# Rotation tables loaded two samples sooner, parted sets ranked ahead, a head's finish one step later, and idle products among the first ones, in a one-core encoder layer

## The chip, the cores and the metric

One core of a Trainium2 chip runs the whole kernel. The metric is the device time of one execution in microseconds (us); the median of three runs is given. A profile of one such execution shows what every engine did: TensorE (PE: matrix products and transposes), VectorE (DVE), ScalarE (ACT), GpSimd (POOL) and SyncE (SP), which here only issues loads and stores.

## What is computed

One layer of a hybrid streaming encoder, for 512 prompt frames and 8 samples of 16 new frames (640 rows of 1024 channels), all in float32:

```
x = x + 0.5 * swiglu(rms_norm(x), ffn1)
z = rms_norm(x) @ w_in_mix            # rq rk rv rg | fq fk fv ff | gates
retention (4 heads): q, k rotated (rotary); o = decayed attention + q @ state; new state
FoX (8 heads): softmax attention with the logit bias sum log f; prompt in blocks of 128,
               samples against 1024 cached frames each
x = x + (g0 * (rms_norm(o_ret) * silu(rg)) @ w_br_ret + g1 * o_fox @ w_br_fox) @ w_out
x = x + 0.5 * swiglu(rms_norm(x), ffn2)
x = x + (p @ w_ple) * sigmoid(rms_norm(x) @ w_ple_gate)
```

## The kernel before

The rows are kept transposed, 640 of them beside each other. Large products are made from weights and inputs that are each split in two parts in a rounded format (ACT casts the first part, `wh`, at L282; DVE makes the rest, `wl`, at L283), as `wh` and `wl` products of 128 x 128 x 320 on PE, all issued by the helper `mm` (L205; transposes are L228). In the mixing part a product of a block of `w_in_mix` is a unit of seven such sums (`MixSeven`), which takes a tile `z1` at its third sum (L822) and `z0` at its fourth (L827), both with the tag `blk`, of which there are 38 slots; the finished rows go to DRAM (`zdram`, `vdram`) on POOL's queue.

These units are the filler. The kernel is written as one order: the mixer's own steps in their turn and, after each step, `fill(us)` issues so many microseconds (by a clock that is kept while the kernel is built) of unit products; `defer` puts a step some time later, `until` runs units up to a name, and `drain` runs all that are left. The builder's order of the instructions follows that order by rank, but takes what is ready. So the stages that matter are, by the time in the profiled execution: FFN 1 (0 to some 480 us); the FoX prompt sweep, `prompt_scores` (L1164) for 2 head groups x 2 pairs x 4 blocks (some 510 to 620); the samples, 8 x 8 steps (`Sample.step`, with its scores, softmax, flips, values and, last, `fold` at L1335 to L1342), to 832; the four retention heads (`Retention`, 832 to some 940, with units between), each with 12 steps; then what follows mixing.

What the change touches: `mm` and its neighbours (L205); the first loop of FFN 1 (`plain[0].products(norm1.ops, j)`, L698; `keep_busy(n, x)`, L253, issues n products of `ones` that nobody reads, into a bank of its own); `prompt_scores`, a set of four products for a pair of heads, two over 40 rows that spread the bias and two over 64 rows, side by side in the array; `Retention.values_s` (L1432), one product and eight over 32 columns each, into one PSUM bank; the sample loop (L1631) and the stretch behind it that loads the tables of retention: `tab` (two tables `c_rope` for `rotate`, L1374), `gqt`, `smt` (`c_smask`, for `scores_s`) and the masks; and `Retention.finish` (ten transposes, products at L1473 and L1474, two stores by POOL). `load` issues on SP's queue, not before a product that lies some time (30 us unless told) earlier by the kept clock.

A tile of a tag takes a slot in the order of the code, and a slot is free when the last reader of the tile before is done. `tmp`, `att`, `big` (in the trace `kv`) and `blk` are such tags in SBUF; `pa` and `pg` are PSUM banks.

Of the kernel before, what the change touches and what calls it, by code (L numbers as in the profile page):

```python
# [19 lines left out]
P = 128  # L20
# [3 lines left out]
NB = 8  # L24
L = 16
# [5 lines left out]
RH, DK, DV = 4, 128, 256  # L31
FH, FD = 8, 64
# [12 lines left out]
LEAD = 30.0  # L45

MERGE_THEN = 5, 1, 1, 0
FILL_P0, FILL_P1, FILL_S0, FILL_S, FILL_R, FILL_B = 1.76, 1.6, 19.8, 10.0, 2.45, 6.4

SM = {}  # L50
# [81 lines left out]
def kernel(  # L132
# [20 lines left out]
    def nm(base):  # L153
        uid[0] += 1
        return f"{base}_{uid[0]}"
# [3 lines left out]
    def blk(shape=(P, T), dt=F32, tag="blk"):  # L159
        n = 1  # L160
        for s in shape[1:]:
            n *= s
        assert n <= T
        return bp.tile(list(shape), dt, tag=tag, name=nm(tag), bufs=slots[tag])
# [4 lines left out]
    def att(dt=F32, shape=(P, 512)):  # L169
        return blk(shape, dt, tag="att")  # L170
# [10 lines left out]
    def tmp(shape=(P, H2), dt=F32):  # L181
        return bp.tile(list(shape), dt, tag="tmp", name=nm("tmp"), bufs=NTMP)
# [4 lines left out]
    def bank(tag="pa"):  # L187
        return pp.tile([P, 512], F32, tag=tag, name=nm(tag), bufs=6 if tag == "pa" else 2)

    def pair(tag="pa"):  # L190
        return [bank(tag), bank(tag)]
# [3 lines left out]
    def tick(inst, us):  # L195

        clock[0] += us
        if not issued or clock[0] - issued[-1][0] > 1.0:
            issued.append((clock[0], inst.ins.name))

    def mm(out, lhsT, rhs, start, stop, **kw):
        n = 1
        for d in rhs.shape[1:]:
            n *= d
        i = nc.tensor.matmul(out, lhsT, rhs, start=start, stop=stop, **kw)  # L205
        tick(i, max(n, 256) / 2400.0 if rhs.dtype == F32R else max(n, 128) / 600.0 * (0.3 if lhsT.shape[-1] <= 32 else 0.5 if lhsT.shape[0] == FD else 1.0))
        return i

    def after(inst, name, why):
        tc.add_manual_dep(inst.ins, name, mybir.DependencyInfo(mybir.DependencyClass.NoSync, mybir.DependencyReason.SCHED_ONLY), reason=why)  # L210

    def load(out, in_, lead=LEAD):

        i = nc.sync.dma_start(out, in_)  # L214
        at = clock[0] - lead
        name = next((nm_ for c, nm_ in reversed(issued) if c <= at), None)
        if name is not None:
            after(i, name, "no tile taken too soon")
# [22 lines left out]
    def flip_gains(n0, n, rows):  # L241
        gb, at = bank("pg"), slice(n0, n0 + n)
        transpose(gb[:, :n * KC], rows)
        nc.vector.tensor_copy(gains[:, at].rearrange("p n c -> p (n c)"), gb[:, :n * KC])
        nc.vector.tensor_scalar(less[:, at], gains[:, at], -1.0, None, op0=ALU.mult)
# [7 lines left out]
    def keep_busy(times, x=None):  # L253

        for _ in range(times):
            nc.tensor.matmul(busy[:, :P], ones, ones if x is None else x[:, :P], start=True, stop=True)
# [395 lines left out]
    with tc.manual_schedule(engines={mybir.EngineType.SP}):  # L652
        for q in range(KC // 2):
            cols = slice(q * 256, (q + 1) * 256)
            xi = big((P, TB, 256))
            n = P if q == 0 else 256
# [16 lines left out]
    xs0 = []  # L673

    def x_in(q):
        for c in (2 * q, 2 * q + 1):
            xc = blk()
            b, b2 = bank(), bank("pg")
            for t in range(TB):
                transpose(b[:, t * P:(t + 1) * P] if t < 4 else b2[:, :P], xins[q][:, t, c % 2 * P:(c % 2 + 1) * P])  # L680
            nc.vector.tensor_copy(xc[:, :S], b)
            nc.scalar.copy(xc[:, S:], b2[:, :P])
            if c == 0:
                keep_busy(4, xc)
            xs0.append(xc)
            norm1.add_parts(c, xc)
            if c % 2 == 0:
                first_parts(norm1.ops, xc[:, H2:], norm1.gain(c), "b12")

    def x_out(q):  # L690
        for c in (2 * q, 2 * q + 1):
            nc.sync.dma_start(xd[0][c], xs0[c])
        norm1.add_square(xins[q], marks[max(q - 1, 0)])

    plain, marks = [Plain(raws[0])], []
    for j in range(KC // 2):
        x_in(j)
        plain[0].products(norm1.ops, j)  # L698
        marks.append(issued[-1][1])
        if j:  # L700
            x_out(j - 1)
        if j == 2:
            flip_gains(1, 3, more)
# [56 lines left out]
    def defer(us, thunk):  # L760
        uid[0] += 1
        heapq.heappush(deferred, (clock[0] + us, uid[0], thunk))

    def pump(everything=False):
        while deferred and (everything or deferred[0][0] <= clock[0]):
            heapq.heappop(deferred)[2]()
# [177 lines left out]
    pick = const.tile([104, FH], F32R, name="pick")  # L944
    c_row = []
# [76 lines left out]
    qk_out = {}  # L1022
# [141 lines left out]
    def prompt_scores(hu, pr, i):  # L1164

        n, both = (i + 1) * P, pair()
        for h2, ps in ((1, both[1]), (0, both[0])):
            head, rows = hu * 4 + 2 * pr + h2, slice(h2 * FD, h2 * FD + 40)
            last = mm(ps[:, :n], pick[rows, head:head + 1].to_broadcast([40, P]), c_row[0][rows, :n], True, False, skip_group_check=True)
        for h2, ps in ((1, both[1]), (0, both[0])):  # L1170
            rows = slice(h2 * FD, (h2 + 1) * FD)
            m = mm(ps[:, :n], qk_out[hu][rows, 0, pr, i * P:n], qk_out[hu][rows, 1, pr, :n], False, True, skip_group_check=True)
            if h2 == 1:
                after(m, last.ins.name, "the pair of heads side by side in the array")
        while values_due:
            values_due.pop(0)(m)
        for h2, ps in enumerate(both):
            prompt_softmax(hu, 2 * pr + h2, i, n, ps)
# [167 lines left out]
    class Retention:  # L1346
# [85 lines left out]
        def values_s(self):  # L1432

            po = bank()
            mm(po[:, :DV], self.at_s, self.vs[4], True, False, skip_group_check=True)
            for j in range(2):
                for pr in range(NB // 2):
                    mm(po[pr * 32:(pr + 1) * 32, :DV], self.qg[:, pr, j, :], self.st[:, 2 * pr + j, :], False, j == 1, skip_group_check=True)
            o, sq = tmp([P, DV]), tmp([P, DV])
            nc.scalar.copy(o, po[:, :DV])  # L1440
            nc.scalar.activation(sq, o, AF.Square, accum_out=self.ms[:, 4:])
            self.o.append(o)
# [136 lines left out]
    merge[-1].begin, merge[-1].middle = embed_begin, fox_fetch  # L1579
    for hd, n in enumerate(MERGE_THEN):  # L1580
        units += [merge.pop(0) for _ in range(n)]
# [13 lines left out]
    def fill(us):  # L1595
        credit[0] += us
        while credit[0] > 0.0:
            at = clock[0]
            if next(feed, feed) is feed:
                clock[0] += credit[0]  # L1600
                credit[0] = 0.0
            credit[0] -= clock[0] - at
            pump()

    def until(what):
        while what not in ready:
            next(feed)
            pump()

    def drain():  # L1610
        for _ in feed:
            pump()
# [15 lines left out]
    samples[0].load(samples[0].k, cache_k)  # L1628
    samples[0].load(samples[0].k, cache_k)
    fill(FILL_B)  # L1630
    for b in range(NB):  # L1631
        defer(2.0, lambda: samples[b].loads(samples[b + 1] if b + 1 < NB else None))
        for n in range(8):
            samples[b].step(n)
            fill((FILL_S if b else FILL_S0) / 8)
    until("rk")
    fill(FILL_B)
    pump(True)
    tab = []
    for n in range(2):  # L1640
        r = blk()
        load(r, c_rope[n])
        tab.append(r)
    gqt, smt = tmp([P, RH, 2, 2 * L]), blk([P, RH, P])
    load(gqt, c_gq)
    load(smt, c_smask)
    masks = [att(shape=(P, RH, P)) for _ in range(2)]
    for n in range(2):
        load(masks[n], c_rmask[n])
    heads = [Retention(hd) for hd in range(RH)]  # L1650
# [3 lines left out]
    fill(6.0)  # L1654
    for hd, r in enumerate(heads):
        for step in (
            lambda: r.rotate(0), lambda: r.rotate(1), lambda: (r.flip(), heads[hd + 1].first_loads() if hd + 1 < RH else None),
            lambda: r.scores(), lambda: r.scores_s(),
            lambda: (r.states_p(), heads[hd + 1].loads() if hd + 1 < RH else None),
            lambda: r.values(0), lambda: r.values(1), lambda: (r.values_s(), r.states()),  # L1660
            lambda: (r.sizes(), until(("rg", hd)), r.gates()),
            lambda: heads[hd + 1].more_loads() if hd + 1 < RH else None, lambda: r.finish(),
        ):
            step()
            fill(FILL_R)
    drain()
    pump(True)

# [4 lines left out]
    for op in range(KC // 2):  # L1673
# [5 lines left out]
        for o in range(2):  # L1679
            n = 2 * op + o  # L1680
            ps = pair()
# [7 lines left out]
    for op in range(KC // 2):  # L1689
        raw = raw_unit(w_out[0][:, op * 256:(op + 1) * 256], KC, 256)  # L1690
        two = []
        for o in range(2):
            xc = blk()
            load(xc, spill[2 * op + o])
            ps = pair("pa")
# [14 lines left out]
    for q in range(2):  # L1710
        for t in range(TB):
            ps = bank("pa" if t % 2 else "pg")
# [23 lines left out]
    for q in range(4):  # L1736
# [15 lines left out]
        for t in range(TB):  # L1752
            ps = bank()
# [41 lines left out]
```

## Time and profile before

| | us |
| --- | --- |
| runs | 1625.13, 1622.28, 1623.24 |
| median | 1623.24 |
| profiled execution, its own time | 1622.67 |
| span of the profiled execution | 1620.9 |
| PE busy | 1609.3 |
| DVE busy | 1164.4 |
| ACT busy | 731.5 |

The span is the time from the first to the last recorded instruction; the execution's own time has some 1.8 us around it. Busy time is the union of an engine's instructions, whose ends on PE are modelled: a stretch at a lower clock counts as busy. The granted clock of PE (1.00 for 2.4 GHz, 0.50 for 1.2 GHz) is therefore read beside it, in windows of the trace. Waits name the instruction that came last before the waiting one could go on.

### The profile page before, as it was taken

How to read it: one execution, taken by the hardware profiler on the slowest of the kernel's cores; microseconds unless marked ns; L12 is line 12 of the kernel's file. 1: busy time of each engine (PE TensorE's matmuls, PEld its weight loads, DVE VectorE, ACT ScalarE, POOL GpSimd, SP SyncE). 2: the span in 40 equal slices, each digit the busy share in tenths (PEclk: the TensorE clock that was granted, in tenths of full speed). 3: DMA queues.
4: the chain of work that ended last, by engine and by line, in shares of the span. 5: the costliest groups of instructions: out<-in, count | busy, mean ns of one | idle time of the engine just before them, and what ended most of it. 6: DMA issues, size and time to landing. Idle time of an engine off the chain costs nothing.

```text
span 1620.9 us, 30289 instructions
## 1 busy us (share of the span) xinstructions
PE 1609.3 (99%) x11979; PEld 1557.3 (96%) x11979; DVE 1164.4 (72%) x2472; ACT 731.5 (45%) x1536; POOL 94.5 (6%) x172
## 2 busy tenths in 40 slices
PE   9999999999999999999999999999999999999998
PEld 8999999999999888988889999999999999999998
DVE  6885786577777755777779886558884787578663
ACT  6552354244454444444434454435653355235432
POOL 0000000000011111000000010001000000000000
PEclk9999999999999999999999999999999999999999
DMA  7244233433542333577775676444234333433431
GB/s 249 78 131 139 96 93 131 145 101 94 178 130 97 111 115 133 209 281 269 279 259 179 202 260 247 151 135 155 79 101 164 100 91 124 144 111 90 172 123 46
DMA packets 205566, 242.88 MB, mean 150 GB/s; under 512 B 10176, under 2 KB 175984, under 8 KB 201328
## 3 DMA queue, kind: packets, MB, share of 16 engines
q1 hardware_dynamic: 193824, 200.07, 38.0%
q0 software_dynamic: 11392, 40.79, 6.3%
q8 instruction: 94, 1.54, 0.4%
q14 instruction: 48, 0.39, 0.1%
q10 hardware_dynamic: 208, 0.08, 0.0%
HBM read 194.89 MB, written 46.03 MB: 149 GB/s over the span
## 4 chain that ended last, share of the span: by engine, by line
PE 96%; DMA 2%; DVE 1%; ACT 1%; issue 0%; SPq 0%; DVEq 0%
PE pa L205 74%; PE pg L205 18%; PE pa L228 4%; DMA kv<-zdram 1%; DMA blk<-in_c_rope_dram 0%; DMA raw<-in_ffn_w_in_dram 0%; ACT tmp L533 0%; PE pg L228 0%; DVE wl L283 0%; ACT wh L282 0%; DMA kv<-in_x_prompt_dram 0%; SPq L214 0%; DVE kv L1487 0%; ACT blk L361 0%; DVE blk L1473 0%
## 5 line engine op out<-in xcount | busy, mean ns | idle before, releaser
L282 ACT CAST wh<-raw 128x512 fp32r<-128x512 f32 (+1 forms) x525 | 316.3, 613 | 506.7 <-PE pa L205 323.5
L205 PE MATMUL pa<-blk,wh 128*128 128x320 f32 x2344 | 511.1, 311 | 1.1 <-ACT wh L282 1.0
L283 DVE TENSOR_TENSOR wl<-raw,wh 128x512 fp32r<-128x512 f32 (+1 forms) x525 | 351.0, 678 | 107.0 <-ACT wh L282 103.6
L205 PEld LDWEIGHTS pa<-blk,wh 128*128 128x128 f32 x2344 | 388.2, 189 | 4.5 <-ACT wh L282 1.5
L205 PE MATMUL pa<-blk,wl 128*128 128x320 f32 x1172 | 344.4, 310 | 0.0
L205 PE MATMUL pa<-kv,wh 128*128 128x320 f32 x1344 | 251.5, 308 | 0.0
L205 PEld LDWEIGHTS pa<-blk,wl 128*128 128x128 f32 x1172 | 216.5, 189 | 0.5 <-DVE blk L830 0.4
L205 PEld LDWEIGHTS pa<-kv,wh 128*128 128x128 f32 x1344 | 210.6, 188 | 0.0
L205 PE MATMUL pg<-blk,wh 128*128 128x320 f32 x768 | 177.3, 316 | 0.2 <-DVE blk L830 0.2
L205 PE MATMUL pa<-blk,blk 128*128 128x320 f32 (+2 forms) x1064 | 168.3, 304 | 0.0
L205 PE MATMUL pa<-kv,wl 128*128 128x320 f32 x672 | 154.6, 308 | 0.0
L205 PEld LDWEIGHTS pa<-blk,blk 128*128 128x128 f32 (+1 forms) x1064 | 151.9, 183 | 0.1
L205 PE MATMUL pg<-wh,blk 128*128 128x256 f32 x768 | 147.6, 286 | 0.0
L205 PEld LDWEIGHTS pg<-blk,wh 128*128 128x128 f32 x768 | 128.2, 188 | 6.0 <-issue 2.4
L205 PEld LDWEIGHTS pg<-wh,blk 128*128 128x128 f32 x768 | 120.4, 188 | 5.1 <-issue 3.8
L205 PE MATMUL pg<-blk,wl 128*128 128x320 f32 x384 | 118.7, 309 | 0.0
L205 PEld LDWEIGHTS pa<-kv,wl 128*128 128x128 f32 x672 | 112.6, 188 | 0.0
L205 PE MATMUL pg<-wl,blk 128*128 128x256 f32 x384 | 108.7, 284 | 0.0
L283 DVE TENSOR_TENSOR blk<-raw,blk 128x512 fp32r<-128x512 f32 x82 | 56.3, 688 | 38.3 <-ACT blk L282 28.0
L205 PE MATMUL pa<-wh,blk 128*128 128x256 f32 (+1 forms) x432 | 82.4, 285 | 0.0
L282 ACT CAST blk<-raw 128x512 fp32r<-128x512 f32 x82 | 50.7, 621 | 62.5 <-DMA raw<-in_ffn_w_in_dram 48.8
L205 PEld LDWEIGHTS pg<-wl,blk 128*128 128x128 f32 x384 | 72.1, 188 | 1.9 <-issue 1.3
(287 smaller groups left out, 2205.1 us busy)
## 6 DMA issues: line engine op xcount, KB each, us to landing
raw<-in_ffn_w_in_dram SPq DMA_DIRECT2D x86, 512.0 KB, 4.8
raw<-in_w_in_mix_dram SPq DMA_DIRECT2D x25, 1024.0 KB, 5.8
raw<-in_ffn_w_out_dram SPq DMA_DIRECT2D x16, 1024.0 KB, 5.2
kv<-in_cache_fox_k_dram SPq DMA_DIRECT2D x16, 1024.0 KB, 7.1
kv<-in_cache_fox_v_dram SPq DMA_DIRECT2D x16, 1024.0 KB, 5.6
blk<-xd SPq DMA_DIRECT2D x48, 320.0 KB, 5.7
xd<-blk POOLq DMA_DIRECT2D x40, 320.0 KB, 2.8
zdram<-blk POOLq DMA_DIRECT2D x24, 320.0 KB, 3.4
```

The source lines that it names most:

```text
L205: i = nc.tensor.matmul(out, lhsT, rhs, start=start, stop=stop, **kw)
L228: tick(nc.tensor.transpose(out, in_, ident[: in_.shape[0], : in_.shape[0]]), 0.11)
L282: nc.scalar.copy(hi, src)
L283: nc.vector.tensor_tensor(lo, src, hi, op=ALU.subtract)
```

## The change

Four things: a name `together()` for "rank what is issued here 300 places ahead", put around the four products of a set in `prompt_scores` and around the nine of `values_s`; eight idle products behind the first group of FFN 1's products; the two tables and `smt` loaded at the start of sample 6 of 0 to 7, and no longer after the last sample; and each head's `finish` issued in the second step of the next head (the last one's after the loop), so that a head has 11 steps with a fill behind each instead of 12.

```
--- before.py
+++ after.py
@@ -45,6 +45,7 @@
 LEAD = 30.0
 
 MERGE_THEN = 5, 1, 1, 0
+SET_AHEAD = 300
 FILL_P0, FILL_P1, FILL_S0, FILL_S, FILL_R, FILL_B = 1.76, 1.6, 19.8, 10.0, 2.45, 6.4
 
 SM = {}
@@ -205,6 +206,10 @@
         i = nc.tensor.matmul(out, lhsT, rhs, start=start, stop=stop, **kw)
         tick(i, max(n, 256) / 2400.0 if rhs.dtype == F32R else max(n, 128) / 600.0 * (0.3 if lhsT.shape[-1] <= 32 else 0.5 if lhsT.shape[0] == FD else 1.0))
         return i
+
+    def together():
+
+        return tc.high_priority(offset=SET_AHEAD)
 
     def after(inst, name, why):
         tc.add_manual_dep(inst.ins, name, mybir.DependencyInfo(mybir.DependencyClass.NoSync, mybir.DependencyReason.SCHED_ONLY), reason=why)
@@ -696,6 +701,8 @@
     for j in range(KC // 2):
         x_in(j)
         plain[0].products(norm1.ops, j)
+        if j == 0:
+            keep_busy(8, xs0[1])
         marks.append(issued[-1][1])
         if j:
             x_out(j - 1)
@@ -1164,14 +1171,15 @@
     def prompt_scores(hu, pr, i):
 
         n, both = (i + 1) * P, pair()
-        for h2, ps in ((1, both[1]), (0, both[0])):
-            head, rows = hu * 4 + 2 * pr + h2, slice(h2 * FD, h2 * FD + 40)
-            last = mm(ps[:, :n], pick[rows, head:head + 1].to_broadcast([40, P]), c_row[0][rows, :n], True, False, skip_group_check=True)
-        for h2, ps in ((1, both[1]), (0, both[0])):
-            rows = slice(h2 * FD, (h2 + 1) * FD)
-            m = mm(ps[:, :n], qk_out[hu][rows, 0, pr, i * P:n], qk_out[hu][rows, 1, pr, :n], False, True, skip_group_check=True)
-            if h2 == 1:
-                after(m, last.ins.name, "the pair of heads side by side in the array")
+        with together():
+            for h2, ps in ((1, both[1]), (0, both[0])):
+                head, rows = hu * 4 + 2 * pr + h2, slice(h2 * FD, h2 * FD + 40)
+                last = mm(ps[:, :n], pick[rows, head:head + 1].to_broadcast([40, P]), c_row[0][rows, :n], True, False, skip_group_check=True)
+            for h2, ps in ((1, both[1]), (0, both[0])):
+                rows = slice(h2 * FD, (h2 + 1) * FD)
+                m = mm(ps[:, :n], qk_out[hu][rows, 0, pr, i * P:n], qk_out[hu][rows, 1, pr, :n], False, True, skip_group_check=True)
+                if h2 == 1:
+                    after(m, last.ins.name, "the pair of heads side by side in the array")
         while values_due:
             values_due.pop(0)(m)
         for h2, ps in enumerate(both):
@@ -1432,10 +1440,11 @@
         def values_s(self):
 
             po = bank()
-            mm(po[:, :DV], self.at_s, self.vs[4], True, False, skip_group_check=True)
-            for j in range(2):
-                for pr in range(NB // 2):
-                    mm(po[pr * 32:(pr + 1) * 32, :DV], self.qg[:, pr, j, :], self.st[:, 2 * pr + j, :], False, j == 1, skip_group_check=True)
+            with together():
+                mm(po[:, :DV], self.at_s, self.vs[4], True, False, skip_group_check=True)
+                for j in range(2):
+                    for pr in range(NB // 2):
+                        mm(po[pr * 32:(pr + 1) * 32, :DV], self.qg[:, pr, j, :], self.st[:, 2 * pr + j, :], False, j == 1, skip_group_check=True)
             o, sq = tmp([P, DV]), tmp([P, DV])
             nc.scalar.copy(o, po[:, :DV])
             nc.scalar.activation(sq, o, AF.Square, accum_out=self.ms[:, 4:])
@@ -1628,7 +1637,15 @@
     samples[0].load(samples[0].k, cache_k)
     samples[0].load(samples[0].k, cache_k)
     fill(FILL_B)
+    tab = []
     for b in range(NB):
+        if b == NB - 2:
+            for n in range(2):
+                r = blk()
+                load(r, c_rope[n])
+                tab.append(r)
+            smt = blk([P, RH, P])
+            load(smt, c_smask)
         defer(2.0, lambda: samples[b].loads(samples[b + 1] if b + 1 < NB else None))
         for n in range(8):
             samples[b].step(n)
@@ -1636,14 +1653,8 @@
     until("rk")
     fill(FILL_B)
     pump(True)
-    tab = []
-    for n in range(2):
-        r = blk()
-        load(r, c_rope[n])
-        tab.append(r)
-    gqt, smt = tmp([P, RH, 2, 2 * L]), blk([P, RH, P])
+    gqt = tmp([P, RH, 2, 2 * L])
     load(gqt, c_gq)
-    load(smt, c_smask)
     masks = [att(shape=(P, RH, P)) for _ in range(2)]
     for n in range(2):
         load(masks[n], c_rmask[n])
@@ -1654,15 +1665,16 @@
     fill(6.0)
     for hd, r in enumerate(heads):
         for step in (
-            lambda: r.rotate(0), lambda: r.rotate(1), lambda: (r.flip(), heads[hd + 1].first_loads() if hd + 1 < RH else None),
+            lambda: r.rotate(0), lambda: (heads[hd - 1].finish() if hd else None, r.rotate(1)), lambda: (r.flip(), heads[hd + 1].first_loads() if hd + 1 < RH else None),
             lambda: r.scores(), lambda: r.scores_s(),
             lambda: (r.states_p(), heads[hd + 1].loads() if hd + 1 < RH else None),
             lambda: r.values(0), lambda: r.values(1), lambda: (r.values_s(), r.states()),
             lambda: (r.sizes(), until(("rg", hd)), r.gates()),
-            lambda: heads[hd + 1].more_loads() if hd + 1 < RH else None, lambda: r.finish(),
+            lambda: heads[hd + 1].more_loads() if hd + 1 < RH else None,
         ):
             step()
             fill(FILL_R)
+    heads[-1].finish()
     drain()
     pump(True)
```

## Rows read from the trace of the kernel before

**Rows 1.** The page: busy time of each engine over the whole span (us, share, instructions), and the chain of work that ended last, by engine.
```profile
PE 1609.3 (99%) x11979; PEld 1557.3 (96%) x11979; DVE 1164.4 (72%) x2472; ACT 731.5 (45%) x1536; POOL 94.5 (6%) x172
...
PE 96%; DMA 2%; DVE 1%; ACT 1%; issue 0%; SPq 0%; DVEq 0%
```

**Rows 2.** The waits of PE over the whole span: engine, tile and line, what was waited for, us in total, times, longest.
```profile
PE pa L205 <- DVE tmp L1335: 2.6, 1, 2.6
PE pg L228 <- DMA kv<-in_x_sample_dram: 1.5, 1, 1.5
...
PE pa L205 <- DVE blk L1473: 0.4, 1, 0.4
```

**Rows 3.** The chain that ended last, in order of time: start, us, what. The piece ahead of the products at 831.75.
```profile
822.05 7.81 DMA blk<-in_c_rope_dram
```

**Rows 4.** The timeline of DVE, 825 to 832 us: start, us, engine, line, operation, out<-in, count, and in brackets the idle time before it and what ended it.
```profile
825.19 0.69 DVE L424 TENSOR_TENSOR raw<-raw 128x512 f32<-128x512 f32 x1
829.88 1.56 DVE L1374 TENSOR_TENSOR kv<-kv,blk 128x640 f32<-128x640 f32 x2 [4.00 <-DMA blk<-in_c_rope_dram]
831.36 0.34 DVE L1335 SCALAR_TENSOR_TENSOR tmp<-pa,ty,sm 128x128 f32<-128x128 f32 x1
```

**Rows 5.** The timeline of PE, 828 to 834 us.
```profile
828.57 0.45 PE L205 MATMUL pg<-blk,wh 128*128 128x320 f32 x2
828.86 0.31 PE L205 MATMUL pg<-blk,wl 128*128 128x320 f32 x1
831.75 0.57 PE L205 MATMUL pa<-sm,tmp 128*128 128x64 f32 x2 [2.59 <-DVE tmp L1335]
...
833.04 0.73 PE L205 MATMUL pa<-blk,wh 128*128 128x320 f32 x2
833.57 0.47 PE L205 MATMUL pa<-blk,wl 128*128 128x320 f32 x1
```

**Rows 6.** Busy time of each engine in stretches of the span (in the columns after the length: busy us and instructions of PE, PEld, DVE, ACT and POOL; then the granted clock of PE, the DMA engines' busy share, GB/s).
```profile
13.00:14.00 1.00, 1.00 (x8) 1.00 (x6) 0.49 (x1) 1.00 (x7) 0.00 (x0) 0.50 1.09 377
760.00:770.00 10.00, 10.00 (x77) 8.93 (x76) 7.55 (x17) 5.38 (x14) 1.08 (x2) 1.00 0.55 179
815.00:832.00 17.00, 14.41 (x157) 13.74 (x157) 8.83 (x19) 6.43 (x17) 1.31 (x2) 1.00 0.99 327
832.00:833.00 1.00, 1.00 (x5) 1.00 (x5) 1.00 (x2) 0.00 (x0) 0.00 (x0) 0.50 1.07 398
834.00:835.00 1.00, 1.00 (x6) 1.00 (x5) 1.00 (x3) 0.00 (x0) 0.00 (x0) 0.50 1.06 329
835.00:836.00 1.00, 1.00 (x8) 1.00 (x7) 1.00 (x2) 0.54 (x2) 0.00 (x0) 0.84 0.70 159
832.00:910.00 78.00, 78.00 (x510) 71.81 (x510) 70.70 (x146) 32.76 (x71) 7.05 (x12) 0.98 0.54 177
```

**Rows 7.** The timeline of SP, which issues the loads: two stretches, about 770 and 812 to 824 us (the duration is that of issuing).
```profile
770.60 5.40 SPq L214 DMA_DIRECT2D kv<-in_cache_fox_v_dram  x2
...
813.95 4.23 SPq L214 DMA_DIRECT2D kv<-zdram  x6
...
822.05 1.16 SPq L214 DMA_DIRECT2D blk<-in_c_rope_dram  x2
```

**Rows 8.** DMA issues of 812 to 827 us: out<-in, engine, count, KB each, median us from issue to landing.
```profile
kv<-zdram SPq DMA_DIRECT2D x3, 320.0 KB, 8.2
...
blk<-in_c_rope_dram SPq DMA_DIRECT2D x2, 320.0 KB, 8.0
```

**Rows 9.** PE's instructions of 783.49 to 803.37 us in groups: line, engine, operation, out<-in, shapes, count, busy us, mean ns, idle before.
```profile
L205 PE MATMUL pg<-blk,wh 128*128 128x320 f32 x33 | 7.9, 313 | 0.0
L205 PE MATMUL pg<-blk,wl 128*128 128x320 f32 x17 | 5.2, 308 | 0.0
...
L205 PE MATMUL pa<-blk,wh 128*128 128x320 f32 x16 | 3.7, 318 | 0.0
L205 PE MATMUL pa<-blk,wl 128*128 128x320 f32 x8 | 2.5, 307 | 0.0
```

**Rows 10.** The timeline of PE at the places of the other parts: the idle products at the start, two pieces of the prompt's score sets, the bias products of sample 7, and the values of the samples in the heads 0 and 1 (64 or 32 behind the operation's first or second number is the part of the array).
```profile
6.44 1.16 PE L256 MATMUL pg<-blk,ones 128*128 128x128 f32 x8 [0.46 <-DVE blk L681]
...
518.91 0.70 PE L205 MATMUL pa<-kv 64*128 64x128 f32 x4
...
533.30 0.91 PE L205 MATMUL pa<-kv 64*128 64x384 f32 x2
...
792.23 0.48 PE L205 MATMUL pa<-blk,blk 128*128 128x512 f32 x1
...
803.37 0.48 PE L205 MATMUL pa<-blk,blk 128*128 128x512 f32 x1
...
850.59 1.59 PE L205 MATMUL pa<-kv,tmp 128*128 128x256 f32 x18
...
898.85 1.15 PE L205 MATMUL pa<-kv,tmp 128*128 128x256 f32 x6
...
906.83 1.68 PE L205 MATMUL pa<-kv,tmp 128*32 128x256 f32 x14
```

**Rows 11.** The timeline of ACT, 550 to 552 us: a copy that empties two PSUM banks.
```profile
550.91 1.06 ACT L1198 COPY att<-pa 128x512 f32<-128x512 f32 x2
```

More of the change, by code (lines that the diff above doesn't have):

```diff
@@ L47 @@
 MERGE_THEN = 5, 1, 1, 0
+SET_AHEAD = 300
 FILL_P0, FILL_P1, FILL_S0, FILL_S, FILL_R, FILL_B = 1.76, 1.6, 19.8, 10.0, 2.45, 6.4
@@ L207, in mm, with together @@
         return i
+    def together():
+        return tc.high_priority(offset=SET_AHEAD)
     def after(inst, name, why):
@@ L698 @@
         plain[0].products(norm1.ops, j)
+        if j == 0:
+            keep_busy(8, xs0[1])
         marks.append(issued[-1][1])
@@ L1166, in prompt_scores @@
         n, both = (i + 1) * P, pair()
[L1167 to L1174, printed above, removed]
+        with together():
+            for h2, ps in ((1, both[1]), (0, both[0])):
+                head, rows = hu * 4 + 2 * pr + h2, slice(h2 * FD, h2 * FD + 40)
+                last = mm(ps[:, :n], pick[rows, head:head + 1].to_broadcast([40, P]), c_row[0][rows, :n], True, False, skip_group_check=True)
+            for h2, ps in ((1, both[1]), (0, both[0])):
+                rows = slice(h2 * FD, (h2 + 1) * FD)
+                m = mm(ps[:, :n], qk_out[hu][rows, 0, pr, i * P:n], qk_out[hu][rows, 1, pr, :n], False, True, skip_group_check=True)
+                if h2 == 1:
+                    after(m, last.ins.name, "the pair of heads side by side in the array")
         while values_due:
@@ L1434, in values_s @@
             po = bank()
[L1435 to L1438, printed above, removed]
+            with together():
+                mm(po[:, :DV], self.at_s, self.vs[4], True, False, skip_group_check=True)
+                for j in range(2):
+                    for pr in range(NB // 2):
+                        mm(po[pr * 32:(pr + 1) * 32, :DV], self.qg[:, pr, j, :], self.st[:, 2 * pr + j, :], False, j == 1, skip_group_check=True)
             o, sq = tmp([P, DV]), tmp([P, DV])
@@ L1630 @@
     fill(FILL_B)
+    tab = []
     for b in range(NB):
+        if b == NB - 2:
+            for n in range(2):
+                r = blk()
+                load(r, c_rope[n])
+                tab.append(r)
+            smt = blk([P, RH, P])
+            load(smt, c_smask)
         defer(2.0, lambda: samples[b].loads(samples[b + 1] if b + 1 < NB else None))
@@ L1638 @@
     pump(True)
[L1639 to L1644, printed above, removed]
+    gqt = tmp([P, RH, 2, 2 * L])
     load(gqt, c_gq)
-    load(smt, c_smask)
     masks = [att(shape=(P, RH, P)) for _ in range(2)]
@@ L1656 @@
         for step in (
-            lambda: r.rotate(0), lambda: r.rotate(1), lambda: (r.flip(), heads[hd + 1].first_loads() if hd + 1 < RH else None),
+            lambda: r.rotate(0), lambda: (heads[hd - 1].finish() if hd else None, r.rotate(1)), lambda: (r.flip(), heads[hd + 1].first_loads() if hd + 1 < RH else None),
             lambda: r.scores(), lambda: r.scores_s(),
@@ L1661 @@
             lambda: (r.sizes(), until(("rg", hd)), r.gates()),
-            lambda: heads[hd + 1].more_loads() if hd + 1 < RH else None, lambda: r.finish(),
+            lambda: heads[hd + 1].more_loads() if hd + 1 < RH else None,
         ):
@@ L1665 @@
             fill(FILL_R)
+    heads[-1].finish()
     drain()
```

## The prediction

> **What bounds the kernel now.** I read the page first: TensorE (PE) is busy in 1609.3 of 1620.9 us and holds 96% of the chain that ends last [rows 1]. So time can come from three places only: stretches in which PE stands, stretches in which it runs at the lower of its two clock levels (2.4 and 1.2 GHz, a granted clock of 1.00 and 0.50), and PE work that needn't be there. Next the waits of PE: the longest is 2.6 us, on the fold product of the last cached sample, which waits for VectorE's (DVE's) L1335; then 1.5 us on the first input rows and 0.4 us on the fold of the heads' outputs at L1473 [rows 2]. The profiled execution took 1622.67 us (span 1620.9 and 1.8 around it), the median of the runs is 1623.24, so 0.57 is added to what I work out on the profiled one.
>
> **The rope stall, step by step.** The chain runs over the two rotation-table loads: the last link before PE goes on is a transfer of 7.81 us that started to issue at 822.05 [rows 3]. DVE ends L424 at 825.19 + 0.69 = 825.88 and stands 4.00 us, until the tables are there at 829.88; two multiplications of the first head's rotate(0) then run, and L1335, the product that PE needs, has its place on DVE behind them, at 831.36 [rows 4]. PE has run out of ready work at 828.86 + 0.3 = 829.16 and starts the fold product at 831.75, 2.59 us later [rows 5]. That isn't all: the granted clock is 0.50 in 832 to 835 and 0.84 in 835 to 836 [rows 6]. Two wh products that took 0.29 from start to next start before the stall take 0.53 behind it (833.04 to 833.57) [rows 5]. Three slices at half speed give half their time back, 1.5 us, and the next 0.16: some 1.7. **The stall's price is 2.59 + 1.7 = 4.3 us.**
>
> With the tables loaded at the start of sample 6, their DMAs stand on SyncE's (SP's) queue about 60 us before they are used. DVE then comes from L424 at 825.88 to rotate(0) at once if the head's own rows are there: the two products take 829.88 to 831.36 = 1.48, L1335 0.34, so the fold's input is ready at 827.7, 1.5 us before PE gets there at 829.16. PE then runs through, and without a pause I see nothing that would lower its clock. I take all 4.3. Bounds: 0 (case C below) to 4.5. On SP's queue the move lets the rmask, state and head loads behind 822.05 go 1.16 us of issue sooner [rows 7], and 0.9 MB leaves a stretch in which the DMA engines are 0.99 busy [rows 6]; that only helps the head's rows.
>
> **Where the loads go.** Two tables of 320 KB [rows 8] and the mask of 128 x 512 fp32, 256 KB, are 0.9 MB; at the 327 GB/s that the full DMA engines reached [rows 6] that is 2.7 us of all DMA engines. Sample 6 begins in 760 to 770, where the DMA share is 0.55, 179 GB/s [rows 6]; SP's queue has its value loads from 770.60 [rows 7]. The queue is in order, so loads behind the tables get up to 2.7 us later. PE uses what they bring one sample (some 20 us) afterwards; nothing PE did there waited for a DMA [rows 2]. That cover makes it 0; without it 2.7.
>
> **The slots.** A second thing moves with the loads: tiles. The tag blk has 38 slots; counted from the code, 35 are held through the samples (16 norm parts, 12 sums of parts, 7 single ones), and each unit of seven products takes two more, z1 and z0, at its third and fourth product. Held since sample 6, the two tables and the mask make 38 without a unit. So the next unit's z1 has to wait for a slot until sample 7's bias products free suft's, at 792.23 and 803.37 [rows 10], some 20 and 30 us later than sample 6's own value loads begin. What waits behind z1 and z0 are that unit's last 24 products, 24 x 0.147 (0.29 for two, above) = 3.5 us; what lies there beside them is the next sample's transposes, scores and values. Between 783.49 and 803.37 the unit products are 74 of PE's instructions [rows 9], 74 x 0.147 = 10.9 us of the stretch's 19.9. Bounds: 0, if other units and the sample's own work close the gap, up to 10.9 + 1.7 of clock if all of them stand. I take +0.5: the order of PE is made when the kernel is built, with the slots known, and has 9 us of other work there.
>
> **Sets that run in parts of the array.** A set (four products over 64 rows, or eight over 32 columns) costs extra when it is entered and left more than once. Values of the samples in head 0: whole, 1.59 us at 850.59. In head 1 it is in two, 1.15 at 898.85 and 1.68 at 906.83, 2.83, of which I put 0.5 down to two state products in the second: some 0.7 more [rows 10]. Head 3 comes in three such pieces. Of the prompt's score sets three are split by their rank alone; the second half of one is the 0.91 at 533.30, for two products; two others, of which the 0.70 at 518.91 is a piece, cost some 0.7 more together by my estimate from such pieces. In others the second half waits for a PSUM bank that ScalarE (ACT) frees, as the copies of 1.06 at 550.91 do [rows 11], and no rank helps those. What rank can mend adds up to 0.7 + 0.9 + 0.7 + some 1.3 (head 3, twice head 1's) = 3.6. On the other side, products ranked 300 ahead start at the first bank or tile that is free, and ten more sets could fall apart at 0.3 to 0.6 each: +4. I take −2.0, nearer to the mendable end because the sets seen whole have all their inputs ready before they start.
> The row shows that leaving and entering costs about half a microsecond. The Trainium skill, page "TensorEngine Tiling (Array Packing)", Key Properties, says that a change of tiling mode makes TensorE drain; the trace agrees with its 0.7. Its section PSUM Bottleneck says that packing speeds TensorE and not the evacuation of PSUM, so that copies may become the limit; by that alone the ranking would give nothing in the prompt's sets and the sum would be 1.5 smaller. The copy at 550.91 bears it out for some sets, and that is case B below.
>
> **A head's finish one step later.** Its transposes, products and two POOL stores per head are the same; they now come after the next head's rotate(0) and not before it, so POOL's queue gets its stores one step of 2.45 us later, and the reload of these rows comes only after all heads. It takes PE off the wait at L1473: at most 0.4 [rows 2]. Four heads have 11 fills instead of 12, so 9.8 us of unit products move behind the last head. Inside the heads DVE is 70.7 of 78 us busy in 832 to 910 [rows 6]; with less PE work beside it DVE could come to lead. Bounds −0.4 to +2; I take −0.2.
>
> **Idle products at the start.** Eight more fp32 products: the four before them (eight passes) took 1.16 at 6.44 [rows 10], so 2.3 us, in a place where PE stands 1.5 for the inputs [rows 2]. They would hold off the products at 10.51 by some 0.8, and those are followed by a wait of their own. The granted clock is 0.50 at 13 to 14, which the filling may lift; but ACT, which makes what PE multiplies, is 1.00 busy in that same slice [rows 6]. Bounds −1 to +1; I take −0.3.
>
> **Sum.** −4.3 + 0 + 0.5 − 2.0 − 0.2 − 0.3 = −6.3: 1622.7 − 6.3 = 1616.4, and with 0.57 for the median **1617.0**.
>
> **Rivals.**
> A, the forecast, with its own range of 1612 to 1620: chance 0.62.
> B, the sets gain nothing or fall apart more, held by banks and not by rank. For it: the copy at 550.91. Against: half of the splits have no such copy. 1617.0 + 2 = 1619.0 up to 1617.0 + 6 = 1623.0; 1621 as its middle. Chance 0.15.
> C, the stall changes its name: rotate(0) needs the head's own rows as well as the tables. The first six of these loads were issued at 813.95 to 818.2 [rows 7], and such loads landed 8.2 us later [rows 8], so by 826.4; DVE would then be free for L1335 at 828.2, still before 829.16. It decides from a landing at 827.4 on, and from 829.9 all of the 4.3 is lost: 1621.3. That the early tables leave these rows more of the DMA engines speaks against it. Also the case that the change doesn't do what it says. Chance 0.08.
> D, slower: units stand for want of a blk slot at 783 to 803. All of the stretch's unit products standing: 10.9 + 1.7 = 12.6 for the 0.5 of the sum, 1617.0 + 12.1 = 1629.1; the one unit's 24 alone, 3.5 + 1.7: 1621.7. Slower than before from some 10 us on. For it: the count of slots leaves none. Against: the builder orders PE with that in view. Chance 0.15.
>
> **How the numbers follow.** About 0.2% (3.2 us) can be told from no change: faster is under 1620.0, slower over 1626.5. Faster: 0.57 of A and 0.03 of B, 0.60. Slower: 0.11 of D and 0.01 of B, 0.12. Same: 0.28. The range reaches from A's low end less 1 (the sets' full 3.6) to 1626: C, B and the half of D lie within, and some 0.2 outside.
>
> **What would show it.** In the profile after: no wait for the rope load on DVE or PE, granted clock 1.00 in the slices behind the fold product of the last sample, and tables issued about 760 to 770 (rope right). Values of the samples in one piece per head, 1.5 to 1.6 each, and fewer lone second halves in the prompt's stage (sets right). No wait of PE at L1473. What would make it wrong: PE idle or at 0.50 between 773 and 803 (D), DVE waiting for kv rows at about 826 (C), or more and shorter sets than before (B).

## The result, and the profile after

The changed kernel takes 1625.49 us (median of 15 runs, 1623.88 to 1629.21), the kernel before 1623.00 (15 runs, 1620.53 to 1626.17): a ratio of 1.0018, with an interval of 1.0010 to 1.0027. By the ratio that is some 2.9 us slower (the two medians lie 2.5 apart) where 6.2 us faster was forecast. The range of 1611 to 1626 holds the time at its upper end; the direction is wrong. The profiled execution took 1624.14 us (span 1622.4), near the low end of its own runs; that of before, 1622.67, lies near the median of its own. So of the 2.9 us the two traces can show 1.5.

The waits of PE after, over the whole span:

```profile
PE pg L233 <- DMA kv<-in_x_sample_dram: 1.3, 1, 1.3
...
PE pa L206 <- ACT blk L366: 1.0, 1, 1.0
PE pa L206 <- ACT att L1274: 0.9, 1, 0.9
PE pa L206 <- DVE att L1395: 0.9, 1, 0.9
PE pa L206 <- ACT blk L358: 0.8, 1, 0.8
PE pg L206 <- DVE blk L843: 0.6, 1, 0.6
PE pg L206 <- ACT tmp L1529: 0.5, 1, 0.5
```

The two waits at which the prediction aimed in the middle of the kernel, L1335 and L1473 of [rows 2], are gone. In their place stand several of 1 us and less, spread from the start to the merging. The wait for the input rows at the start is still there. The timeline of DVE at the place of [rows 4], and the windows of after where the clock was 0.50 in [rows 6]:

```profile
817.89 0.35 DVE L1343 SCALAR_TENSOR_TENSOR tmp<-pa,ty,sm 128x128 f32<-128x128 f32 x1 [0.27 <-PE pa L206]
...
819.88 0.82 DVE L1382 TENSOR_TENSOR kv<-kv,blk 128x640 f32<-128x640 f32 x1 [0.87 <-DMA kv<-zdram]
```
```profile
13.00:14.00 1.00, 1.00 (x11) 1.00 (x10) 0.44 (x1) 0.68 (x2) 0.00 (x0) 1.00 1.10 379
832.00:833.00 1.00, 1.00 (x9) 1.00 (x9) 0.80 (x2) 1.00 (x3) 0.00 (x0) 1.00 1.05 408
```

rotate(0) starts at 819.88, 10 us sooner than in [rows 4]; the wait ahead of it is 0.87 for the head's own rows, no longer for the tables, and no wait of PE in the list above hangs on it. The granted clock is 1.00 in both places.

Where the time went is read best by stage. The cuts are the starts of four DVE instructions that every kernel here has: the first of the mixing (L1099 of before), the first of the new frames' scores (L1157), the copy of the last fold (L1342) and the last product of the first merging (L1685). Microseconds of each stage in the profiled executions:

| | FFN 1 | prompt | samples | heads, first merging | the rest | span |
| --- | --- | --- | --- | --- | --- | --- |
| before | 452.7 | 181.6 | 202.3 | 227.7 | 556.6 | 1620.9 |
| after | 454.0 | 181.3 | 198.9 | 231.4 | 556.8 | 1622.4 |
| tables | 452.9 | 181.6 | 199.5 | 227.7 | 556.6 | 1618.3 |
| sets | 452.8 | 181.4 | 201.5 | 230.9 | 556.1 | 1622.7 |
| idle | 453.9 | 181.6 | 201.8 | 228.6 | 556.7 | 1622.5 |
| finish | 451.9 | 181.6 | 203.6 | 235.8 | 555.9 | 1628.8 |
| no_finish | 453.8 | 181.3 | 199.6 | 233.4 | 556.2 | 1624.3 |
| fill_r_250 | 452.5 | 181.6 | 202.3 | 233.0 | 557.0 | 1626.4 |
| light_no_finish | 453.8 | 181.3 | 198.8 | 230.0 | 556.0 | 1619.9 |

The change loses 1.3 us at the start, wins 0.3 in the prompt's stage and 3.4 in the samples', and gives 3.7 back between the heads and the end of the first merging. A part of the last two is only work on the other side of a cut: PE has 1911 instructions in the samples' stage of after and 1923 in that of before, and 1563 and 1555 in the heads' stage; eight products at the 0.147 us of the prediction would be 1.2 us, by estimate. PE's idle time in the heads' stage is 2.55 us in after and 0.58 in before, so 2.0 of the 3.7 are PE standing.

### The profile page after: what moved, and what is told of

The parts are those of the page before. It is cut to its first block, busy times and chain, and to the rows that moved or that the text cites. A ratio compares the mean times of both kernels' runs of the same rounds, so it can differ in the third digit from the quotient of the medians.

```text
span 1622.4 us, 30332 instructions
## 1 busy us (share of the span) xinstructions
PE 1609.1 (99%) x11995; PEld 1555.4 (96%) x11995; DVE 1160.5 (72%) x2472; ACT 730.5 (45%) x1536; POOL 94.7 (6%) x172
## 4 chain that ended last, share of the span: by engine, by line
PE 88%; issue 5%; DVE 3%; DMA 3%; ACT 1%; POOL 0%; SPq 0%; POOLq 0%; DVEq 0%; ACTq 0%
PE pa L206 70%; PE pg L206 14%; PE pa L233 3%; DMA kv<-zdram 1%; DVE wl L288 1%; DMA raw<-in_w_br_fox_dram 0%; DMA raw<-in_ffn_w_in_dram 0%; ACT tmp L538 0%; DMA out_dram<-kv 0%; ACT wh L287 0%; PE pg L233 0%; DMA kv<-in_x_prompt_dram 0%; POOL zdram L850 0%; DVE kv L1496 0%; DVE kv L1384 0%
```

## The experiments

Each ratio is to the kernel before, measured on the same chip. The first four make one part of the change each.

**tables**, **sets**, **idle**, **finish**:

```
tables: + if b == NB - 2: tab = the two tables, smt = the mask   (and none behind the samples)
sets:   + with together(): round the set in prompt_scores and in values_s
idle:   + if j == 0: keep_busy(8, xs0[1])
finish: + heads[hd - 1].finish() in the step of rotate(1); 11 steps per head
```

> The early tables alone, all else as before. Theory 1 (the rope stall goes and nothing takes its place; the loss of the whole change is elsewhere): 2.6 us of waiting and the half clock behind it go, some 4 us faster than before, ratio 0.997 to 0.998. Rival 2 (the tables hold slots of the tag blk from sample 6 on, so units and the sample's scores come later and PE waits near 800 to 825): most of it is given back, under 1.5 us faster, with waits of PE in 780 to 830 that before doesn't have. Rival 3 (the stall changes its name): no change, DVE waits for kv rows at about 826.

> The ranking of the two kinds of sets alone. Theory 1: the sets cost some 2 us less in all (0.6 in the prompt's stage, 1.4 in the heads, by the trace of after), so 1 to 2.5 us faster. Rival: the ranking makes other products late, so that waits appear in the heads; within 1 us of before or slower.

> The eight idle products alone. In the trace of after everything behind the first 30 us comes 1.4 us later than before. Theory 1 (the idle products take PE's time and what they fill isn't worth it): 1 to 1.8 us slower, all of it in the first 30 us. Rival (the start's delay in after was of that execution alone, and a clock that stays up pays for them): within 0.6 us of before.

> The finish one step later alone. Theory 1 (with 11 fills instead of 12 per head the heads run with less PE work beside DVE's, DVE and the loads of the head's rows come to lead there, and the last units' chains lie bare behind the heads): 2 to 5 us slower, with waits of PE in 900 to 1000. Rival 2 (the loss is the slots' or the ranking's): within 1 us of before.

| | median us | ratio | interval |
| --- | --- | --- | --- |
| tables | 1620.58 | 0.9985 | 0.9976 to 0.9994 |
| sets | 1623.17 | 1.0001 | 0.9993 to 1.0010 |
| idle | 1624.31 | 1.0008 | 1.0000 to 1.0017 |
| finish | 1630.43 | 1.0041 | 1.0026 to 1.0056 |

The tables alone are 2.4 us faster, between the 4 of theory 1 and the 1.5 of rival 2. The samples' stage of the trace is 2.8 shorter, and rival 2 names what took a part of the rest. The timeline of ACT at the copy to z1, first in before, then in tables, and that of PE in tables near 810:

```profile
771.72 0.42 ACT L823 COPY blk<-pg 128x320 f32<-128x320 f32 x1
```
```profile
790.19 0.43 ACT L823 COPY blk<-pg 128x320 f32<-128x320 f32 x1
```
```profile
810.27 1.06 PE L205 MATMUL pa<-att,blk 128*32 128x512 f32 x8 [0.94 <-ACT att L1266]
```

z1 is made 18.5 us later, right behind sample 7's first bias product (at 792.23 in [rows 10], at 789.42 in tables), which lets a slot go, and the sample's scores, whose own work now runs ahead of the unit's products, wait 0.94 us. Later the first merging waits; here the chain of tables, and PE's timeline with 1.56 us of it:

```profile
960.26 18.31 DMA blk<-retd
```
```profile
980.63 0.56 PE L205 MATMUL pg<-blk,wh 128*128 128x320 f32 x2 [1.56 <-DVE blk L1550]
```

The sets alone give nothing. The sets themselves take some 2.0 us less in the trace of after than in that of before, by adding up their pieces (the samples' values over 32 columns stand in seven pieces in before and in four, one for each head, in after); but the sets run has waits of 1.8 and 1.3 in the heads and the merging that before doesn't have. The idle products cost 1.3, at the edge of what the interval can tell. In the trace of before PE stood 1.5 for the inputs [rows 2]; here is PE's timeline in after, and behind it the copy on DVE that makes the part of the tile `xs0[1]` that the idle products multiply:

```profile
8.52 0.31 PE L206 MATMUL pa<-blk,wl 128*128 128x320 f32 x1
10.11 0.30 PE L233 MATMUL pg<-sm,kv 128*128 128x128 f32 x1 [1.28 <-DMA kv<-in_x_sample_dram]
10.25 1.95 PE L261 MATMUL pg<-blk,ones 128*128 128x128 f32 x16
11.95 1.13 PE L206 MATMUL pa<-blk,wh 128*128 128x320 f32 x6
```
```profile
8.14 0.68 DVE L686 COPY blk<-pa 128x512 f32<-128x512 f32 x1
```

The products stand behind the wait, not in it: 1.28 us of it remain, and then 1.95 us of products that nobody reads. Their input was there at 8.14 + 0.68 = 8.82, just as the wait began; but in PE's order they come after the transpose at 10.11, which waits for the next rows. The finish alone costs 6.7 us, the most of all, and more than the 2 to 5 of theory 1. Beside the wait for the rope, which is 3.5 in its trace, its waits of PE are spread over the heads and the first merging:

```profile
PE pg L205 <- ACT tmp L820: 2.0, 2, 1.3
PE pg L205 <- ACT tmp L1520: 1.5, 2, 0.9
PE pg L205 <- DVE blk L833: 1.4, 1, 1.4
PE pa L205 <- DVE att L1414: 1.1, 1, 1.1
```

L820 and L833 are steps between one sum of a unit and the next; the three waits on them stand at 916, 934 and 966. That units have less work beside them there fits theory 1, but isn't shown by it. The sum of the four is +5.8 us, that of the whole +2.9. The parts don't add.

**finish_12**, **fills_11**, **tables_7**, **no_finish** take the parts apart further:

```
finish_12: finish, and a twelfth step that does nothing (lambda: None) with its fill
fills_11:  before, r.finish() behind the loop over the steps, without a fill behind it
tables_7:  tables, loaded behind samples[7].step(4)
no_finish: the whole change without the part finish
```

> The finish one step later alone, with an empty twelfth step in each head so that the 12 fills per head of before stay. Theory 4 (what costs 6.7 us in the finish run is the four missing fills: 9.8 us of units less beside the heads and bare behind them): the loss goes, within 1.5 us of before. Rival 5 (the place of the finish costs: its eight DVE products and stores among the next head's rotation): still over 4 us slower.

> The kernel before with the finish in its old place, and only the fill behind it left out, so 11 fills per head. Theory 4 (the missing fills): 4 to 8 us slower than before, with waits of PE in 920 to 985 as in the finish run. Rival 5 (the place of the finish): within 1.5 us of before.

> The early tables alone, but loaded behind the fifth step of sample 7 (some 15 us before their use), when both bias tiles of the samples have given their slots back. Theory 6 (in the tables run z1 had to wait 18 us for a slot, and that gave back some 1.5 of the 4 us of the rope stall): the copy to z1 stands where it stood before, no wait of PE near 810, and 3.5 to 4.5 us faster than before. Rival (the missing part of the gain has nothing to do with slots): 2 to 3 us faster, as in the tables run, or less because the loads come later.

> The whole change but for the finish, which stays in its old place with 12 fills. Theory 1 (the parts add, and the finish is the loss): the single runs give -2.4 + 0.2 + 1.4 = -0.8, so 0 to 2 us faster than before. Rival (the parts disturb each other, and the finish mends some of it in the company of the others): no faster than the whole change, 2 us or more slower than before.

| | median us | ratio | interval |
| --- | --- | --- | --- |
| finish_12 | 1627.72 | 1.0031 | 1.0019 to 1.0043 |
| fills_11 | 1630.02 | 1.0046 | 1.0034 to 1.0058 |
| tables_7 | 1625.11 | 1.0019 | 1.0011 to 1.0028 |
| no_finish | 1625.09 | 1.0016 | 1.0007 to 1.0024 |

All four contradict a theory of single prices. The missing fills alone cost 7.5 us (theory 4), and yet with the fills put back the finish still costs 5.0 (rival 5): either is enough. tables_7 has z1 at its old place, 771.84, and no wait near 810, as theory 6 said, but it is 3.1 us slower than before where 3.5 to 4.5 faster was expected. In its trace PE waits 1.6 for the state of head 3 at 975 and then runs at 0.50 for 3.4 us. And without the finish the whole change is as slow as with it: in that company the finish costs some 0.3 us, less than the intervals, not 6.7. The trace of no_finish shows a place where time is lost. Its timeline of PE there:

```profile
977.07 1.07 PE L206 MATMUL pa<-kv,tmp 128*32 128x256 f32 x16 [0.61 <-DMA kv<-in_state_ret_dram]
981.21 0.90 PE L206 MATMUL pg<-blk,wh 128*128 128x320 f32 x2 [3.07 <-DVE blk L1559]
```

its chain ahead of that, and its windows (clock, DMA share and GB/s are the last three columns):

```profile
953.55 7.06 DMA blk<-zdram
...
968.23 10.93 DMA blk<-retd
```
```profile
960.00:980.00 20.00, 17.06 (x118) 13.82 (x116) 9.72 (x29) 6.86 (x14) 7.51 (x14) 1.00 1.05 403
...
982.00:984.00 2.00, 2.00 (x9) 2.00 (x8) 1.14 (x4) 1.97 (x7) 0.00 (x0) 0.50 0.09 33
```

The DMA engines are full in 960 to 980. Before has the same there, with PE busy throughout; the whole change has it too, and PE stands in it for 1.24 us (the same window, first of before, then of after):

```profile
960.00:980.00 20.00, 20.00 (x144) 19.45 (x143) 13.27 (x33) 7.97 (x16) 6.81 (x12) 1.00 1.05 403
```
```profile
960.00:980.00 20.00, 18.76 (x123) 16.61 (x122) 13.47 (x34) 10.16 (x23) 8.21 (x15) 1.00 1.04 397
```

In that stretch the reloads of the heads' outputs (retd) and gates (zdram), the weights of the merging, the last head's state and POOL's stores all meet. The next four ask whether that is the cause, and how fine the setting is.

**light_before**, **light_no_finish**, **tables_sets**, **fill_r_250** (light leaves the new states of seven of the eight samples in the heads 2 and 3 out of the output):

```
light:       - nc.gpsimd.dma_start(o_state_s[0, :, hd]..., self.st)
             + n = NB if hd < 2 else 1
             + nc.gpsimd.dma_start(o_state_s[0, :n, hd]..., self.st[:, :n])
tables_sets: before with the parts tables and sets
fill_r_250:  before with FILL_R 2.45 -> 2.5
```

> The kernel before, with the new states of heads 2 and 3 stored for one of the eight samples only (the output leaves out the other seven): 1.8 MB less to DRAM, half of it in 955 to 985, the rest as before. Theory 7 (the DMA engines are full at 955 to 985, and what the change wins ahead of it is lost there in waits for reloads): before has no such wait there, so little to win, 0 to 1 us faster.

> The no_finish kernel with the same stores cut (the output leaves out the new states of seven samples in heads 2 and 3). Theory 7 (DMA engines full at 955 to 985): 0.9 MB at 400 GB/s is 2.2 us, so the wait of 3.1 us for the reload of retd falls under 1 us, the half clock behind it goes, and it comes 3 to 6 us faster than no_finish, to 0 to 3 us faster than before. Rival (the wait comes from the order of PE and DVE, not from bytes): within 1 us of no_finish, 2 us slower than before.

> The early tables and the ranked sets, without the idle products and with the finish in its old place. If the parts add: -2.4 + 0.2, so some 2 us faster than before. If they meet at the reloads of 955 to 985 as in the no_finish run (which is this and the idle products): +2.4 - 1.4, so some 1 us slower than before.

> The kernel before with nothing of the change, and the fill behind each step of the heads 2.50 us and not 2.45: 48 x 0.05 = 2.4 us of units moved from behind the heads into them. Theory 8 (the stretch from the heads to the merging is set so finely that any shift of a few us costs, whatever its kind): 1.5 to 5 us slower, with waits of PE in 900 to 1000 that before doesn't have. Rival (only what the change moves costs): within 1 us of before.

| | median us | ratio | interval |
| --- | --- | --- | --- |
| light_before | 1623.75 | 0.9999 | 0.9990 to 1.0008 |
| light_no_finish | 1622.41 | 0.9991 | 0.9983 to 1.0000 |
| tables_sets | 1623.13 | 0.9997 | 0.9989 to 1.0006 |
| fill_r_250 | 1629.53 | 1.0035 | 1.0021 to 1.0048 |

The smaller stores do nothing for before and take 4.1 us (1.0016 to 0.9991) off no_finish, whose waits on the reload fall from 3.3 to 1.2 us, in two each, with no half clock behind. The full stretch is over sooner as well: the DMA share is 0.91 in 975 to 980 and 0.18 in 980 to 985, for 1.05 and 0.41 in no_finish. So bytes bear on it; that they are all of it isn't shown. The smaller stores also change PE's order: the two traces have another instruction at 228 of 11995 places, all behind 960. And another order can cost as much by itself: fill_r_250, which has nothing of the change and differs from before at 499 places, all behind 900, is 5.7 us slower, more than the 1.5 to 5 of theory 8; the heads' stage takes 233.0 in place of 227.7. Before stands low in this stage, at least for a step to this side; a smaller fill was not tried. tables_sets reached neither the sum of its parts nor before's heads' stage.

Four more, all beside the whole change:

```
light_after:    the whole change with the stores of light
no_idle:        the whole change without keep_busy(8, xs0[1])
after_fill_267: the whole change with FILL_R 2.673 (11 x 2.673 = 12 x 2.45)
no_sets:        the whole change without together()
```

> The whole change with the new states of heads 2 and 3 stored for one of eight samples only (the output leaves out the other seven). Theory 7 (full DMA engines at 955 to 985): 2 us or more faster than the whole change, about at before or better. Rival (in the whole change the loss is the order of PE and DVE in the heads, with the finish among the rotation): within 1 us of the whole change.

> The whole change without the eight idle products. If their cost stays at the start and adds: 1.4 us faster than the whole change, some 1 us slower than before. If a shift of a microsecond is as good as any other (theory 8), anything from 2 us faster to 3 us slower than the whole change.

> The whole change with a fill of 2.673 in place of 2.45 behind each step of the heads, so that the 11 fills of a head hold what 12 held before. If the missing fills cost in this company what they cost alone: 3 to 6 us faster than the whole change. Theory 8 (before's setting was a fine low point and any other is worse): within 2 us of the whole change, on either side.

> The whole change without the ranking of the sets. If the ranking's price of 2 us less in the sets is all it does: 2 us slower than the whole change. If what it saves is lost in waits behind it, as in the sets run: within 1 us of the whole change.

| | median us | ratio | interval |
| --- | --- | --- | --- |
| light_after | 1623.66 | 1.0003 | 0.9994 to 1.0011 |
| no_idle | 1621.19 | 0.9990 | 0.9981 to 0.9998 |
| after_fill_267 | 1624.82 | 1.0013 | 1.0002 to 1.0024 |
| no_sets | 1626.69 | 1.0024 | 1.0014 to 1.0033 |

light_after is 2.4 us faster than the whole change, as theory 7 had it, but the intervals touch, and the two traces (heads' stage 231.4 and 230.5) don't show where; here too PE's order differs, at 271 places. So the full stretch may hold a part of what the change gave back; how much isn't shown. no_idle is 4.5 us faster than the whole change and 1.6 faster than before, outside of both that was expected: the idle products cost 1.3 alone and 4.5 in company. The 1.3 is their price at the start: FFN 1 takes 453.1 to 454.3 us in the traces of the seven kernels that have them and 451.9 to 452.9 in those of the eleven that don't. The rest isn't theirs directly: leaving them aside, the orders of PE in no_idle and in the whole change differ at 288 places, all but six between 940 and 1020, while before and idle differ at six in all. So some 3 us come with another order of the merging, with the same bytes moved. The ranking, worth nothing alone, would save 1.0 in company (1.0024 to 1.0018), which the intervals can't tell from nothing. after_fill_267 is inside 2 us of the whole change, as theory 8 had it, and not 3 to 6 faster.

In no_idle the time differs from one execution to the next, and its trace shows where it can be lost. Its profiled execution took 1624.65 us, the longest of its twelve (1619.99 to 1624.65) and 3.5 over their median. It carries one long wait of PE at that place, and a lower clock behind it (waits of PE, then windows):

```profile
PE pg L206 <- ACT tmp L1527: 3.9, 1, 3.9
...
PE pa L206 <- ACT blk L358: 1.2, 2, 0.9
```
```profile
966.00:968.00 2.00, 0.12 (x1) 0.12 (x2) 0.41 (x1) 1.06 (x3) 0.00 (x0) 1.00 1.03 420
...
970.00:972.00 2.00, 2.00 (x6) 1.60 (x5) 1.02 (x3) 0.00 (x0) 0.00 (x0) 0.50 0.96 357
```

The Trainium skill, page "DMA: Bandwidth & Descriptors", section "Issuing engines are not separate DMA queues", says that transfers issued by the scalar, sync or gpsimd engine end up on the same 16 DMA engines and interleave. The runs agree, as far as they part bytes from order: with POOL's stores cut by 2 x 0.9 MB, PE's waits for what SP reloads fell from 3.3 to 1.2 us.

## Why the prediction was wrong

**The rope stall: right in mechanism, and not the end of it.** The wait at L1335, the half clock behind it and the rope wait of DVE are gone; tables alone won 2.8 us in the samples' stage, the whole change 3.4, of the 4.3 forecast. It isn't the luck of one trace: the stage takes 198.7 to 199.8 us in the nine kernels with the tables at sample 6 and 201.5 to 203.6 in the eight with the tables in their old place. Part of what is missing is the slots' term, right in mechanism as well: z1 came 18.5 us later in tables and a wait of 0.94 arose. The prediction priced it at +0.5; case D, with all units standing, did not come about, since the order let the sample's own work go first. Case C did not come about: the head's rows came in time but for 0.87 us of DVE.

**The step that failed** is the sum itself: it takes what a stage wins as won at the end. The prediction set the moves after 832 at −0.2 for the finish and had no term for what the other parts do to the heads and the merging. Few waits of PE there [rows 2] look like room. It was the reverse: this stage takes 3.7 us more in the trace of after. The DMA engines are full from 960 to 980 in before as well, and a shift of 0.05 us in each fill makes the stage 5.3 us longer in its trace. Of the seventeen other kernels all but tables, idle and after_fill_267 have it over 2 us longer than before in their traces (a single trace can mislead: light_before has it 3.0 longer, and its median is that of before). How much of the loss is the full DMA engines and how much the order of the instructions stays open. The views to read for it were at hand: the DMA share by windows behind the heads, not only ahead of them.

**The sets:** 0.6 us less in the prompt's sets and 1.4 in the heads', so −2.0 was met in the sets themselves. Case B, no gain, came true for the time, but mostly not by its reason: one set at least stays apart (the second pick of the set at 550.09 in after still comes 2.8 us behind the first), yet the sets got shorter, and what they won went in waits behind: 0.0 in all when alone, −1.0 in company, within the intervals.

**The idle products:** the wrong step was "2.3 us, in a place where PE stands 1.5 for the inputs". PE's order has them behind the instruction that waits, though their input was there at 8.82, so the wait stayed and 1.95 us were added: +1.3 for −0.3. The half clock at 13 to 14 of [rows 6] comes and goes without them: the traces of tables, sets and finish don't have it, that of fill_r_250 has it.

**The finish:** forecast at −0.2 with a bound of +2, it cost 6.7 alone, and some 0.3 in company. Each half of it costs by itself, the place 5.0 and the missing fills 7.5; that is shown. Why the two together cost no more than one, and why the parts don't add, is not settled: it was not tried to hold the order of all engines fixed while one part changes, which the kernel's way of ordering does not allow.

**Chances.** Slower had 0.12, for slots (case D) and the sets alone. A case "what is won ahead is lost where the DMA engines are full behind the heads" was missing; that the range holds the time is luck: it was drawn wide for other reasons.

Of all kernels here tables is the fastest, 0.9985 of before, with no_idle next at 0.9990; their intervals overlap. Both are faster than the whole change and the kernel before.

## What to carry to other kernels

Removing a stall pays only what the stages behind it don't take back: look at the DMA share and at what PE waits for in every stage behind it, and take a stage in which nothing waits as one that may just fit. Before a part is credited or blamed, measure a control that moves the same stage by a trifle (here a fill of 2.50 for 2.45 us: 5.7 us), because a tuned order may answer to any shift, and compare the orders of the two traces. An idle product fills a wait only if it stands ahead of the waiting instruction in its engine's order; that its input is there in time is not enough.

## What the runs showed of the hardware

A wait of PE can cost more than its length, and its length alone doesn't tell: behind waits of 2.59 (before), 3.07 (no_finish) and 3.9 us (no_idle) PE ran at a granted clock of 0.50 for 3.4, 6.8 and 3.4 us, and behind 1.6 us in tables_7 and 2.0 us in idle for 3.4; behind those of 1.56 (tables), 1.8 (sets) and 2.6 us (tables_sets) it stayed at 1.00. A reload of 320 KB of retd, of which the median between 940 and 985 is 6.1 us, took 18.31 us in the tables run, 9.83 of them for its issue on SP's queue.
